# Halved feed-forward products: one more pair per layer, and the last part of layer 1's second projection

## The chip, the cores and the metric

The kernel runs on one core of a Trainium2 chip. The time is device microseconds of one execution. Before the change the runs took 1472.92, 1473.97 and 1474.12 us, a median of 1473.97.

## What is computed

A trunk of two layers on 512 positions of width 1024, all in float32. Each layer normalizes, mixes (a gated convolution with differential attention in layer 0, stick-breaking attention in layer 1), attends to 256 memory positions, and ends in a gated feed-forward part:

```python
def conv_ffn(h, w_up, w_conv, w_down):
    u = causal_dwconv(h @ w_up, w_conv)
    gate, val = jnp.split(u, 2, axis=-1)
    return (jax.nn.silu(gate) * val) @ w_down
...
    x = x + conv_ffn(rmsnorm(x, norm_ffn[l]), ffn_w_up[l], ffn_conv[l], ffn_w_down[l])
```

`w_up` is 1024 x 5632, `w_down` 2816 x 1024, and `w_conv` has width 3 over positions. Only this part is changed.

## The kernel before

Activations lie with features on the 128 partitions and the 512 positions along a row, in tiles ("k tiles") of 128 features. Every float32 operand is carried as two reduced-precision parts, hi (a cast, on ACT) and lo (the rest, a subtraction on DVE, in `split`), and a product is three matmuls: hi with hi, hi with lo, lo with hi.

**Groups.** The weights are cut into groups, listed in the order in which PE uses them by `weight_groups`. In a feed-forward part U0 to U21 are the up-projections: Uj gives one tile of gates and one of values from 8 k tiles. The down-projection is cut by its 22 k tiles into D0 (k tiles 0 to 7, groups D00 to D03 of two output tiles each), D1 (8 to 15, D10 to D13) and D2 (16 to 21, D20 and D21 of four output tiles). `FFN_ORDER` mixes them. A plain U is 2 x 8 x 3 = 48 matmuls of 512 columns; D2 is 8 x 6 x 3 = 144.

**Halved groups.** `lin_halved` takes a U group as a 2 x 2 block product (even and odd k tiles, gate and value, first and second 256 positions) from seven block products instead of eight: 7 x 4 x 3 = 84 matmuls of 256 columns. It needs sums of activations, T, made by `fold`: the scaled activations S of the 8 k tiles and, for each pair of them, two tiles of sums. It also needs sums of weight blocks: the load "a" holds two blocks as they are, "d" one, "b" and "c" sums. The seven products p1 to p7 go to PSUM tiles acc, sc, pv, tr, sc, tr, sc, from which DVE combines the four output quarters c11 to c22 in the tiles u1 and u2. There are 2 sc and 2 tr buffers and one pv, so DVE's reading frees what PE writes next. U7 to U21 of both layers are halved (`SEVEN`); U0 to U5 use unscaled activations and scale the result afterwards (`UP_SCALED`), U6 uses the scaled ones whole.

**Weight sums.** `sums_in_dram` makes b and c ahead of time in DRAM: one copy of the group's four blocks (1 MB, in the queue of SP, "dr<-wts 16x16384"), then three adding copies in POOL's queue (512, 256 and 256 KB). `SUMMED` says after which group each sum is started. `halved_loads` then loads a, d, b, c into the 3 raw buffers; `prep_halved` splits them into the 5 hi and 5 lo buffers (d into sq). SP's queue is in order: a load that waits for a raw buffer holds everything behind it.

**Lo parts by POOL.** For the groups in `LOW` (U2 to U6) lo is not made by DVE: ACT writes the negated hi and POOL adds the weights to it with an adding copy.

**The order.** The program has no fixed order of its own. The class `Issue` plans, when it is built, which instruction of which stream comes next on each engine, from costs (`act`, `tt`, `mm`, `dma`, `add_dma`) and priorities (a smaller number first: 0.9 for the combinations, 1.0 for what follows a product, `FOLD` for fold, 3.0 for loads and splits, `SUMS` for the weight sums). The order of every engine is then fixed in the program.

The end of layer 1: D21's last output tile is added to x and written out in two halves of 256 positions.

Of the kernel before, what the change touches and what calls it, by code (L numbers as in the profile page):

```python
# [17 lines left out]
P = 128  # L18
# [19 lines left out]
UP_SCALED = 6  # L38
FFN_ORDER = [('u', 0), ('u', 1), ('u', 2), ('u', 3), ('u', 4), ('u', 5), ('u', 6), ('u', 7), ('d', 0, 0), ('u', 8), ('d', 0, 1), ('u', 9), ('u', 10), ('d', 0, 2), ('u', 11), ('u', 12), ('d', 0, 3), ('u', 13), ('u', 14), ('u', 15), ('u', 16), ('d', 1, 0), ('u', 17), ('d', 1, 1), ('u', 18), ('d', 1, 2), ('u', 19), ('u', 20), ('d', 1, 3), ('u', 21), ('d', 2, 0), ('d', 2, 1)]
SEVEN = {0: (7, 8, 9, 10, 11, 12, 13, 14, 15, 16, 17, 18, 19, 20, 21), 1: (7, 8, 9, 10, 11, 12, 13, 14, 15, 16, 17, 18, 19, 20, 21)}  # L40

SUMMED = {0: {7: 'A1', 8: 'A1', 9: 'A2', 10: 'A2', 11: 'EO0', 12: 'EO0', 13: 'EO1', 14: 'KV1_0', 15: 'KV3_0', 16: 'Q0_0', 17: 'Q0_0', 18: 'Q1_0', 19: 'XO0_0', 20: 'XO0_0', 21: 'XO1_0'}, 1: {7: 'U17_0', 8: 'U19_0', 9: 'U21_0', 10: 'SQK0', 11: 'SQK0', 12: 'SV0', 13: 'SQK1', 14: 'SQK2', 15: 'SV1', 16: 'SQK3', 17: 'Q0_1', 18: 'Q1_1', 19: 'XO0_1', 20: 'XO1_1', 21: 'U1_1'}}


def weight_groups():
# [22 lines left out]
    def common(l):  # L68
        for a in range(2):
            g.append((f"Q{a}_{l}", "x_w_q", l, ks, c(*range(4 * a, 4 * a + 4))))  # L70
        for a in range(2):
            g.append((f"XO{a}_{l}", "x_w_out", l, ks[4 * a:4 * a + 4], c(*range(8))))

        def up(j):
            g.append((f"U{j}_{l}", "ffn_w_up", l, ks, c(j, 22 + j)))

        def dn(a, b):
            kk = list(range(8 * a, min(8 * a + 8, 22)))
            n = 2 if a < 2 else 4
            g.append((f"D{a}{b}_{l}", "ffn_w_down", l, kk, c(*range(n * b, n * b + n))))  # L80

        for step in FFN_ORDER:
            (up if step[0] == "u" else dn)(*step[1:])
# [21 lines left out]

LOW = {GN[n] for n in ('U2_0', 'U2_1', 'U3_0', 'U3_1', 'U4_0', 'U4_1', 'U5_0', 'U5_1', 'U6_0', 'U6_1')}
# [3 lines left out]
NSLOT = [len(g[3]) * len(g[4]) * P // SLOT for g in GROUPS]  # L110
FIRST = [sum(NSLOT[:i]) for i in range(len(GROUPS) + 1)]
# [38 lines left out]

PREP_FIRST, SUM_FIRST, SUM = 0.45, 3.2, 1.5

FOLD = 1.4

# [51 lines left out]
def vw(x):  # L206
    return x.v() if isinstance(x, T) else x
# [182 lines left out]
def trunk(ctx: ExitStack, tc: tile.TileContext, xT: bass.AP, memT: bass.AP, wts: bass.AP, par: bass.AP, outT: bass.AP):  # L390
# [259 lines left out]
    extra = {}  # L650

    def blocks(gi):

        return wts[FIRST[gi]:FIRST[gi] + 2].rearrange("s p c -> (s p c)").rearrange("(b p c) -> b p c", b=4, p=P)

    summed = {}

    def sums_in_dram(gi, after):

        yield Until(lambda: fin.get(after, 0) > 0)  # L660
        x = blocks(gi)
        d = yield AL(pDR, F32, (4, P, 512))
        yield dma(d.v(), x, 2 * SLOT)
        yield add_dma(d[0:2], x[1:3])
        yield add_dma(d[2], d[0])
        yield add_dma(d[3], d[2])
        summed[gi] = d

    def halved_loads(gi):
        x = blocks(gi)  # L670
        take = [("a", x[0:4:3]), ("r", x[1:3])]
        if gi in ADDED:
            yield Until(lambda: gi in summed)
            d = summed[gi]
            take = [("a", x[0:4:3]), ("d", x[2:3]), ("b", d[1:3]), ("c", d[0:4:3])]
        for n, src in take:
            w = 512 if n == "d" else SLOT
            raw = yield AL(pRAW, F32, (P, w), parts=w // 512)
            v = raw.v().re("p (b c) -> p b c", c=512)
# [25 lines left out]
    def prep_halved(gi):  # L705

        pair = [AL(pHI, F32R, (P, SLOT), parts=2), AL(pLO, F32R, (P, SLOT), parts=2)]
        half = [AL(pSQ, F32R), AL(pSQ, F32R)]
        if gi in ADDED:
            for n in "adbc":  # L710
                yield Until(lambda: (gi, n) in raws)
                r = raws[gi, n]
                h, lo = yield half if n == "d" else pair
                if gi in LOW7 and n in "bc":
                    yield act(h, r)
                    yield act(lo, r, scale=-1.0)
                    src = summed[gi][slice(1, 3) if n == "b" else slice(0, 4, 3)].re("b p c -> p b c")
                    yield add_dma(V(lo, lo.h.rearrange("p (b c) -> p b c", c=512)), src)
# [9 lines left out]
        prepped[gi, "a"] = (ha, la)  # L728
        a11, a12, a21, a22 = r0[:, :512].p(0), r0[:, 512:].p(1), r1[:, :512].p(0), r1[:, 512:].p(1)
        hd, ld = yield half  # L730
# [72 lines left out]

    def lin_halved(gi, N, acc, done):

        st = {}
        t1, t2 = slice(0, 256), slice(256, 512)

        def product(ps, slot, off, rhs, last=True):
            for q in range(4):  # L810
                yield Until(lambda: (gi, slot) in prepped and N.get("folded", 0) > q)
                hi, lo = prepped[gi, slot]
                j = off // 512
                cs = slice(off + q * P, off + (q + 1) * P)
# [31 lines left out]
        def neg(out, a, ps):  # L846
# [5 lines left out]
        then(act(c11, acc[:, :256]), lambda: free(acc), flag("p1"))  # L852
        p2 = yield AL(aSC)
        yield from product(p2[:, :256], "a", 512, part(1, t1))
        p4 = yield AL(aPV)
        yield from product(p4[:, :256], "d", 0, sums(1, t1))
        p6 = yield AL(aTR)
        yield from product(p6[:, :256], "b", 512, sums(1, t2), last=False)
        then(Until(lambda: "p1" in st), sub(c12, c11, p6), lambda: free(p6), flag("p6"),
             add(c11, c11, p2), lambda: free(p2))  # L860
        p5 = yield AL(aSC)
        yield from product(p5[:, :256], "b", 0, sums(0, t1))
# [5 lines left out]
        p3 = yield AL(aSC)  # L868
        yield from product(p3[:, :256], "c", 512, part(1, t2))
        then(Until(lambda: "p5" in st), add(c12, c12, p3), lambda: free(p3), lambda: done(0, u1))  # L870
        fin[gi] = 2
# [591 lines left out]
    def ffn(l, xin, xout, last):  # L1463
        N = norm_x(xin, f"norm_ffn{l}", True)
        acts, own, gate_t = {}, {}, {}

        def fold():

# [9 lines left out]
            for q in range(4):  # L1478
# [4 lines left out]
                for k, b in ((2 * q, b1), (2 * q + 1, b2)):  # L1483
# [9 lines left out]
                    N["S"][k] = (hi, lo)  # L1493
                x, y, z, w = b1[:, t1].p(0), b1[:, t2].p(1), b2[:, t1].p(0), b2[:, t2].p(1)
                yield tt(x, y, x, ALU.subtract)
                yield tt(y, w, y, ALU.subtract)
                yield tt(w, w, x, ALU.subtract)
                yield tt(z, z, w, ALU.subtract)
                for b, (hi, lo) in zip((b1, b2), N["T"][q]):
                    yield from split(hi, lo, b)  # L1500
                free(b1, b2)
# [47 lines left out]
        def dn(a, b):  # L1549
            n = 2 if a < 2 else 4  # L1550
            base = add_x(names[a], names[a + 1], n * b)

            def done(m, ps):
                k = n * b + m
                if last and a == 2 and k == KD - 1:

                    yield Until(lambda: (names[a], k) in F)
                    x = F[names[a], k]
                    for js in (slice(0, S // 2), slice(S // 2, S)):
                        yield tt(x[:, js], x[:, js], ps[:, js], ALU.add)  # L1560
# [309 lines left out]
```

## Time and profile before

| what | value |
|---|---|
| median of the runs | 1473.97 us |
| the profiled execution, its own time | 1473.73 us |
| its span | 1471.9 us |
| granted clock | 1.00 |
| POOL busy | 168.5 us (11%) |
| layer 0, U0 starts, U7 starts, U21 ends | 374.2, 451.3, 689.8 us |
| layer 1, U0 starts, U7 starts, U21 ends, D21 ends | 1119.6, 1196.8, 1435.3, 1468.0 us |
| memory read, written | 239.9, 65.0 MB |

PE is TensorE's matmuls, PEld its weight loads, which overlap them, DVE VectorE, ACT ScalarE, POOL GpSimd, SP SyncE with the queue of the loads. The starts and ends of groups are those of their matmuls in the trace, times are counted from the start of the span, and an operation is written out<-in. q1 is the hardware queue that SP fills, q0 the software queue that POOL fills. DMA shares are of the core's 16 DMA engines. The lines themselves stand in the prediction, where they are used.

### The profile page before, as it was taken

To read this page: it belongs to the slowest core of one execution; us is meant where nothing else is said; L and a number is where in the kernel's file an instruction comes from. 1 tells how busy PE (TensorE), PEld (TensorE's weight loads), DVE (VectorE), ACT (ScalarE), POOL (GpSimd) and SP (SyncE) were. 2 spreads that over 40 slices of the span, in tenths; PEclk is the share of its full clock that TensorE was granted. 3 is DMA by queue.
4 is the path that set the end of the run, shared out by engine and by line. 5 is a ranking of instruction groups with operands and counts; after the bars stand their busy time and mean duration, and the time that the engine had idled before them with its cause. 6 is when DMAs were issued, how large, how long until landed. Compare 5 with 4: busy or idle time off the path is not lost.

```text
span 1471.9 us, 21459 instructions
## 1 busy us (share of the span) xinstructions
PE 1465.0 (100%) x8048; PEld 1272.2 (86%) x8048; DVE 1113.1 (76%) x1891; ACT 810.7 (55%) x1335; POOL 168.5 (11%) x249
## 2 busy tenths in 40 slices
PE   9999999999999999999999999999999999999998
PEld 8888888888889999999888888888888889999897
DVE  7689766665798788867687989967656996888683
ACT  6576546453675445444477877855535854545341
POOL 3212121211210000000111111001101300000000
PEclk9999999999999999999999999999999999999999
DMA  6128898967784445658465463453547954455351
GB/s 237 58 86 243 224 264 269 255 169 161 178 177 143 144 151 170 200 169 227 158 154 147 122 187 79 137 178 107 148 126 219 224 149 128 144 159 184 117 165 57
DMA packets 86088, 243.41 MB, mean 165 GB/s; under 512 B 8064, under 2 KB 8576, under 8 KB 85504
## 3 DMA queue, kind: packets, MB, share of 16 engines
q1 hardware_dynamic: 63744, 200.09, 40.2%
q0 software_dynamic: 22240, 41.95, 17.6%
q8 instruction: 63, 1.03, 0.3%
q14 instruction: 41, 0.34, 0.1%
HBM read 239.91 MB, written 65.01 MB: 207 GB/s over the span
## 4 chain that ended last, share of the span: by engine, by line
PE 95%; DVE 2%; ACT 2%; DMA 1%; issue 1%; SPq 0%; DVEq 0%; ACTq 0%
PE acc L492 67%; PE sc L492 13%; PE pv L492 6%; PE tr L492 6%; PE tr L496 3%; DVE lo L454 0%; ACT h L439 0%; DMA raw<-wts 0%; ACT g L442 0%; DMA x<-xT 0%; DVE g L1619 0%; DVE h L454 0%; DVE g L454 0%; DVE c L454 0%; ACT pt L439 0%
## 5 line engine op out<-in xcount | busy, mean ns | idle before, releaser
L492 PE MATMUL acc<-hs,hi 128*128 128x512 f32 x1568 | 493.7, 392 | 0.0
L439 ACT CAST hi<-raw 128x1024 fp32r<-128x1024 f32 (+1 forms) x294 | 303.3, 1038 | 211.1 <-PE acc L492 79.8
L454 DVE TENSOR_TENSOR lo<-raw,hi 128x1024 fp32r<-128x1024 f32 (+1 forms) x274 | 328.7, 1205 | 90.7 <-ACT hi L439 89.5
L492 PEld LDWEIGHTS acc<-hs,hi 128*128 128x128 f32 x1568 | 292.4, 188 | 57.7
L492 PE MATMUL acc<-hs,lo 128*128 128x512 f32 x784 | 307.5, 392 | 0.0
L492 PE MATMUL acc<-hi,hs 128*128 128x512 f32 x544 | 175.4, 395 | 0.3 <-ACT hs L442 0.3
L492 PEld LDWEIGHTS acc<-hs,lo 128*128 128x128 f32 x784 | 147.3, 188 | 28.7
L492 PE MATMUL acc<-h,hi 128*128 128x512 f32 (+1 forms) x600 | 170.2, 368 | 0.0
L454 DVE TENSOR_TENSOR x<-x,acc 128x512 f32<-128x512 f32 (+1 forms) x105 | 71.2, 680 | 71.4 <-PE acc L492 71.1
L492 PEld LDWEIGHTS acc<-h,hi 128*128 128x128 f32 x600 | 108.2, 189 | 18.1
L462 DVE SCALAR_TENSOR_TENSOR g<-c,pp,g 128x511 f32<-128x511 f32 (+1 forms) x168 | 116.9, 745 | 2.5 <-ACT g L442 2.4
L492 PEld LDWEIGHTS acc<-hi,hs 128*128 128x128 f32 x544 | 100.9, 188 | 20.3 <-ACT hs L442 0.6
L492 PE MATMUL acc<-h,lo 128*128 128x512 f32 (+1 forms) x300 | 109.5, 368 | 0.0
L492 PE MATMUL acc<-lo,hs 128*128 128x512 f32 x272 | 106.8, 393 | 0.0
L492 PE MATMUL acc<-y,hi 128*128 128x512 f32 (+1 forms) x280 | 74.2, 346 | 0.0
L508 POOL DMA_DIRECT2D dr<-wts x30 | 27.4, 913 | 392.1 <-DMA dr<-wts 385.6
L442 ACT ACTIVATE g<-c,pp 128x512 f32<-128x512 f32 x84 | 58.1, 719 | 19.1 <-DVE c L454 18.9
L454 DVE TENSOR_TENSOR g<-g,g 128x512 f32<-128x512 f32 (+2 forms) x112 | 62.9, 568 | 5.0 <-ACT g L439 2.0
L492 PEld LDWEIGHTS acc<-h,lo 128*128 128x128 f32 x300 | 56.6, 189 | 9.4
L442 ACT ACTIVATE g<-sc,rq 128x128 f32<-128x128 f32 (+7 forms) x128 | 61.2, 537 | 5.4 <-PE sc L492 4.9
L508 POOL DMA_DIRECT2D dr<-dr x60 | 50.3, 848 | 115.3 <-DMA dr<-wts 70.1
L492 PEld LDWEIGHTS acc<-lo,hs 128*128 128x128 f32 x272 | 51.2, 188 | 10.0
(241 smaller groups left out, 2672.1 us busy)
## 6 DMA issues: line engine op xcount, KB each, us to landing
raw<-wts SPq DMA_DIRECT2D x226, 512.0 KB, 4.2
raw<-dr SPq DMA_DIRECT2D x60, 512.0 KB, 3.7
dr<-wts POOLq DMA_DIRECT2D x30, 512.0 KB, 6.1
dr<-dr POOLq DMA_DIRECT2D x60, 256.0 KB, 4.7
lo<-wts POOLq DMA_DIRECT2D x20, 512.0 KB, 7.8
raw<-wts SPq DMA_DIRECT2D x38, 256.0 KB, 3.1
x<-xT SPq DMA_DIRECT2D x16, 256.0 KB, 4.7
raw<-memT SPq DMA_DIRECT2D x4, 512.0 KB, 4.5
```

Source lines behind the costliest of these rows:

```text
L439: return nc.scalar.copy(out=out.ap, in_=in_.ap)
L442: return nc.scalar.activation(out=out.ap, in_=in_.ap, func=func, scale=_raw(scale), **kw)
L454: lambda: _ve(eng).tensor_tensor(out=out.ap, in0=in0.ap, in1=in1.ap, op=op))
L462: lambda: nc.vector.scalar_tensor_tensor(out=out.ap, in0=in0.ap, scalar=_raw(scalar), in1=in1.ap, op0=op0, op1=op1))
L492: lambda: nc.tensor.matmul(out.ap, lhsT.ap, rhs.ap, start=start, stop=stop))
L496: return Op("PE", 0.109, [in_, ident_v], [out], lambda: nc.tensor.transpose(out.ap, in_.ap, ident_v.ap))
L508: lambda: nc.gpsimd.dma_start(out=out.ap, in_=i, accum_op=ALU.add, max_dma_last_dim=2048))
```

## The change

1. U6 is halved in both layers, 16 groups of each layer in place of 15, and leaves `LOW`.
2. D2 of layer 1 is four halved groups D20 to D23 in place of two plain ones, each with two output tiles and 6 k tiles: 7 x 3 x 3 = 63 matmuls of 256 columns, 252 together in place of 144 of 512. `fold_down` adds hi and lo of the activations 16 to 21 and makes their sums T (in buffers of kl and pt, free once U6 to U21 are done). The weight blocks have 384 columns (`width`), and their sums are made in DRAM like the others. p5 goes to acc, and p4 of D21 and D23 too. In D23 p2 comes last, and `end` adds to x and writes out the first output tile in two halves.
3. Each layer has its own `FFN_ORDER`. Layer 1 has U17, U18, D11, U19, U20, U21, D12, D13 and then D2.
4. `FOLD` goes from 1.4 to 0.8, and `SUM`, a priority in the norms, from 1.5 to 0.7.
5. `SUMMED` starts the sums at other places. Up to the feed-forward part of layer 0, 12 are started in place of 15; in it 13 (U18 to U21 of layer 0, U6 to U14 of layer 1) in place of 3; between the two parts 3 in place of 12; in layer 1's part 8 (U18 to U21, D20 to D23, after U8 to U13).

```diff
+SEVEN_DOWN = (1,)
+SEVEN = {0: (6, 7, 8, 9, 10, 11, 12, 13, 14, 15, 16, 17, 18, 19, 20, 21), 1: (6, 7, 8, 9, 10, 11, 12, 13, 14, 15, 16, 17, 18, 19, 20, 21)}
...
+DOWN_AFTER = {'D20_1': 'U9_1', 'D21_1': 'U10_1', 'D22_1': 'U12_1', 'D23_1': 'U13_1'}
...
-PREP_FIRST, SUM_FIRST, SUM = 0.45, 3.2, 1.5
-FOLD = 1.4
+PREP_FIRST, SUM_FIRST, SUM = 0.45, 3.2, 0.7
+FOLD = 0.8
...
+    def width(gi):
+        return len(GROUPS[gi][3]) // 2 * P
...
+        p4 = yield AL(aACC if GROUPS[gi][0][:2] == "D2" and GROUPS[gi][0][2] in "13" else aPV)
...
+        p5 = yield AL(aSC if GROUPS[gi][0][0] == "U" else aACC)
...
+        if end is not None:
+            p2 = yield AL(aSC)
+            yield from product(p2[:, :256], "a", 1, part(1, t1))
+            spawn(end(None, p2), 0.8)
...
+        def sums_of(b1, b2, out):
+            t1, t2 = slice(0, 256), slice(256, 512)
+            x, y, z, w = b1[:, t1].p(0), b1[:, t2].p(1), b2[:, t1].p(0), b2[:, t2].p(1)
+            yield tt(x, y, x, ALU.subtract)
+            yield tt(y, w, y, ALU.subtract)
+            yield tt(w, w, x, ALU.subtract)
+            yield tt(z, z, w, ALU.subtract)
+            for b, (hi, lo) in zip((b1, b2), out):
+                yield from split(hi, lo, b)
+
+        def fold_down():
+            yield lin_done(*(f"U{j}_{l}" for j in range(UP_SCALED, 22)))
...
+            for q in range(3):
+                b1, b2 = yield [AL(pC, parts=2), AL(pC, parts=2)]
+                for k, b in ((16 + 2 * q, b1), (17 + 2 * q, b2)):
+                    yield Until(lambda: k in acts)
+                    hi, lo = (vw(x) for x in acts[k])
+                    yield tt(b, hi.f32(), lo.f32(), ALU.add)
+                    ND["S"][k - 16] = acts[k]
+                yield from sums_of(b1, b2, ND["T"][q])
+                free(b1, b2)
+                ND["folded"] = q + 1
...
+            def end(u, p2):
+                k = n * b
+                x = F[names[a], k]
+                t1, t2 = slice(0, 256), slice(256, 512)
+                if p2 is None:
+                    yield tt(x, x, u, ALU.add)
+                    free(u)
+                    F["end"] = True
+                    yield dma(outT[k][:, t2], x[:, t2], 256)
+                else:
+                    yield Until(lambda: "end" in F)
+                    yield tt(x[:, t1], x[:, t1], p2[:, :256], ALU.add)
+                    free(p2)
+                    yield dma(outT[k][:, t1], x[:, t1], 256)
...
+        if l in SEVEN_DOWN:
+            spawn(fold_down(), 1.2)
```

Where rows move, three places. First SP's queue in layer 0 during U13 to U15, with the loads for U15 and U16. Before:

```order
159 L501 DMA raw_5568<-wts 128x2x512
160 L501 DMA raw_5584<-wts 128x512
161 L501 DMA raw_5605<-dr_2655 128x2x512
162 L501 DMA raw_5653<-dr_2655 128x2x512
163 L501 DMA raw_5704<-wts 128x2x512
164 L501 DMA raw_5731<-wts 128x512
165 L501 DMA raw_5759<-dr_2759 128x2x512
166 L501 DMA raw_5792<-dr_2759 128x2x512
167 L501 DMA raw_5841<-wts 128x1024
```

These are a, d, b, c of U15, then of U16, then the first load of D10. With the change, the same loads:

```order
164 L507 DMA raw_5641<-wts 128x2x512
165 L507 DMA raw_5657<-wts 128x512
166 L507 DMA raw_5679<-dr_2755 128x2x512
167 L507 DMA dr_5701<-wts 16x16384
168 L507 DMA raw_5730<-dr_2755 128x2x512
169 L507 DMA raw_5781<-wts 128x2x512
170 L507 DMA raw_5809<-wts 128x512
171 L507 DMA dr_5842<-wts 16x16384
172 L507 DMA raw_5838<-dr_3053 128x2x512
173 L507 DMA raw_5873<-dr_3053 128x2x512
174 L507 DMA raw_5923<-wts 128x1024
```

Two copies for weight sums of layer 1 (U8 and U9, the rows dr<-wts) have come between the loads, one ahead of U15's c and one ahead of U16's b.

Second, DVE where fold ends in layer 0 (pt and rrow are its last sums, acc_4228 and acc_4275 are U6's results, g_4171 and g_4179 the convolutions of U3 and U4). Before:

```order
640 L462 SCALAR_TENSOR_TENSOR g_4360<-acc_4228,pp,g_4360 128x511
641 L454 TENSOR_TENSOR pt_3856<-c_4264,pt_3856 128x512
642 L454 TENSOR_TENSOR hs_4373<-g_4323,hs_4372 128x512
643 L462 SCALAR_TENSOR_TENSOR g_4360<-acc_4228,pp,g_4360 128x510
644 L454 TENSOR_TENSOR rrow_3858<-c_4265,pt_3856 128x512
645 L454 TENSOR_TENSOR lo_4385<-raw_4318,hi_4384 128x1024
646 L454 TENSOR_TENSOR lo_4409<-raw_4339,hi_4408 128x1024
647 L462 SCALAR_TENSOR_TENSOR g_4407<-acc_4275,pp,g_4407 128x511
```

With the change:

```order
619 L468 SCALAR_TENSOR_TENSOR g_4171<-c_4120,pp,g_4171 128x511
620 L460 TENSOR_TENSOR pt_3832<-c_4127,pt_3832 128x512
621 L460 TENSOR_TENSOR rrow_3834<-c_4128,pt_3832 128x512
622 L468 SCALAR_TENSOR_TENSOR g_4171<-c_4120,pp,g_4171 128x510
623 L468 SCALAR_TENSOR_TENSOR g_4179<-c_4169,pp,g_4179 128x511
624 L460 TENSOR_TENSOR g_4171<-g_4171,g_4092 128x512
625 L468 SCALAR_TENSOR_TENSOR g_4179<-c_4169,pp,g_4179 128x510
626 L460 TENSOR_TENSOR c_4217<-acc_4093,rrow_3822 128x512
627 L460 TENSOR_TENSOR h_4225<-g_4171,h_4225 128x512
```

Fold's last two rows have moved from U6's convolutions to those of U3 and U4.

Third, DVE at the end of the program. Before, from the adds of D12 on (lo_14622 is the split of D21's last weights):

```order
1869 L454 TENSOR_TENSOR x_1838<-x_1838,acc_14381 128x512
1870 L454 TENSOR_TENSOR x_1840<-x_1840,acc_14425 128x512
1871 L454 TENSOR_TENSOR x_1842<-x_1842,acc_14443 128x512
1872 L454 TENSOR_TENSOR lo_14622<-raw_14473,hi_14621 128x1024
1873 L454 TENSOR_TENSOR x_1845<-x_1845,acc_14601 128x512
1874 L454 TENSOR_TENSOR x_1852<-x_1852,acc_14606 128x512
1875 L454 TENSOR_TENSOR x_1859<-x_1859,acc_14616 128x512
1876 L454 TENSOR_TENSOR x_1866<-x_1866,acc_14641 128x512
1877 L454 TENSOR_TENSOR x_1872<-x_1872,acc_14662 128x256 x2
```

With the change, from the last product of D20 (sc_14850) to the split of D22's a weights:

```order
1924 L460 TENSOR_TENSOR c_14766<-c_14766,sc_14850 128x256
1925 L460 TENSOR_TENSOR c_14767<-pv_14778,c_14767 128x256
1926 L460 TENSOR_TENSOR x_1838<-x_1838,c_14766 128x512
1927 L460 TENSOR_TENSOR x_1840<-x_1840,c_14767 128x512
1928 L460 TENSOR_TENSOR lo_14848<-raw_14819,hi_14847 128x768
```

and the last rows, all of D23, where tr_15103 is p7, acc_15090 p5, sc_15114 p3, acc_15061 p4 and sc_15125 p2:

```order
1957 L460 TENSOR_TENSOR c_15060<-acc_15090,c_15060 128x256
1958 L460 TENSOR_TENSOR c_15059<-c_15059,sc_15114 128x256
1959 L460 TENSOR_TENSOR c_15060<-acc_15061,c_15060 128x256
1960 L460 TENSOR_TENSOR x_1866<-x_1866,c_15059 128x512
1961 L460 TENSOR_TENSOR x_1872<-x_1872,c_15060 128x512
1962 L460 TENSOR_TENSOR x_1866<-x_1866,sc_15125 128x256
```

Where DVE had an add for each output tile, it now combines products, adds and splits ahead of the next group; and behind the last two products stand five rows in place of two.

More of the change, by code (lines that the diff above doesn't have):

```diff
@@ L109 @@
 HALVED = {GN[f"U{j}_{l}"] for l in SEVEN for j in SEVEN[l]}
-NSLOT = [len(g[3]) * len(g[4]) * P // SLOT for g in GROUPS]
+HALVED |= {GN[f"D2{b}_{l}"] for l in SEVEN_DOWN for b in range(4)}
+DOWN_AFTER = {'D20_1': 'U9_1', 'D21_1': 'U10_1', 'D22_1': 'U12_1', 'D23_1': 'U13_1'}
+ADDED.update({GN[n]: GN[after] for n, after in DOWN_AFTER.items()})
+NSLOT = [-(-len(g[3]) * len(g[4]) * P // SLOT) for g in GROUPS]
 FIRST = [sum(NSLOT[:i]) for i in range(len(GROUPS) + 1)]
@@ L705, in prep_halved @@
     def prep_halved(gi):
-        pair = [AL(pHI, F32R, (P, SLOT), parts=2), AL(pLO, F32R, (P, SLOT), parts=2)]
-        half = [AL(pSQ, F32R), AL(pSQ, F32R)]
+        w = width(gi)
+        pair = [AL(pHI, F32R, (P, 2 * w), parts=2), AL(pLO, F32R, (P, 2 * w), parts=2)]
+        half = [AL(pSQ, F32R, (P, w)), AL(pSQ, F32R, (P, w))]
         if gi in ADDED:
@@ L868, in lin_halved @@
         p3 = yield AL(aSC)
-        yield from product(p3[:, :256], "c", 512, part(1, t2))
-        then(Until(lambda: "p5" in st), add(c12, c12, p3), lambda: free(p3), lambda: done(0, u1))
+        yield from product(p3[:, :256], "c", 1, part(1, t2))
+        then(Until(lambda: "p5" in st), add(c12, c12, p3), lambda: free(p3),
+             (lambda: done(0, u1)) if end is None else (lambda: spawn(end(u1, None), 0.9)))
+        if end is not None:
+            p2 = yield AL(aSC)
+            yield from product(p2[:, :256], "a", 1, part(1, t1))
+            spawn(end(None, p2), 0.8)
         fin[gi] = 2
@@ L1493, in fold @@
                     N["S"][k] = (hi, lo)
[L1494 to L1500, printed above, removed]
+                yield from sums_of(b1, b2, N["T"][q])
                 free(b1, b2)
@@ L1573, in fr @@
                         free(*own[j])
+                    if a == 2 and l in SEVEN_DOWN:
+                        free(*ND["own"])
                 spawn(fr(), 0.1)
```

81 lines of the change are left out of this document (42 added, 39 removed).

## The prediction

> **What bounds the kernel now.** I read the busy times and the chain on the page first, then the waits of PE.
>
> ```profile
> PE 1465.0 (100%) x8048; PEld 1272.2 (86%) x8048; DVE 1113.1 (76%) x1891; ACT 810.7 (55%) x1335; POOL 168.5 (11%) x249
> PE 95%; DVE 2%; ACT 2%; DMA 1%; issue 1%; SPq 0%; DVEq 0%; ACTq 0%
> PE pv L492 <- POOL pt L514: 1.1, 1, 1.1
> PE tr L496 <- DVE pt L454: 0.7, 1, 0.7
> PE sc L492 <- DVE s L1096: 0.5, 1, 0.5
> PE acc L492 <- ACT hs L442: 0.3, 1, 0.3
> PE sc L492 <- ACT g L442: 0.3, 1, 0.3
> ```
>
> PE is 95% of the chain that ended last and waits 2.9 us in all (the last five rows: total, times, longest). So the time is the sum of the matmuls, and anything that makes PE wait is added to it. The feed-forward parts are where the change is made, and there PE has two possible suppliers that could come late: DVE and the weight loads. The stretches of the four products U13 to U16 of layer 0, one row each (engines' busy us, then clock, DMA share, GB/s), behind one row for all of U7 to U21 of that layer:
>
> ```profile
> 451.40:689.80 238.40, 238.40 (x1646) 223.24 (x1645) 184.94 (x282) 111.72 (x149) 5.09 (x6) 1.00 0.56 172
> 555.40:565.50 10.10, 10.10 (x86) 10.10 (x85) 5.61 (x10) 3.53 (x5) 0.00 (x0) 1.00 0.40 131
> 565.50:575.50 10.00, 10.00 (x86) 10.00 (x84) 9.35 (x15) 6.11 (x10) 0.00 (x0) 1.00 0.52 166
> 575.50:585.60 10.10, 10.10 (x87) 10.10 (x86) 10.10 (x18) 6.57 (x10) 0.00 (x0) 1.00 0.62 183
> 585.60:595.70 10.10, 10.10 (x87) 10.10 (x86) 10.10 (x18) 5.77 (x9) 0.00 (x0) 1.00 0.59 176
> ```
>
> In the last two rows DVE (third engine) is busy 10.10 of 10.10 us. These are the places where four products of 10.1 us stand in a row with no down-projection between. A DVE that is held up there has nothing to catch up with, and PE follows closely behind it (DVE rows, and one of PE, us from the start and length):
>
> ```profile
> 576.18 0.42 DVE L454 TENSOR_TENSOR c<-sc,c 128x256 f32<-128x256 f32 x1
> 576.52 0.41 DVE L454 TENSOR_TENSOR c<-c,sc 128x256 f32<-128x256 f32 x1
> 576.94 0.40 PE L492 MATMUL sc<-y,hi 128*128 128x256 f32 x2
> 577.18 1.22 DVE L454 TENSOR_TENSOR lo<-raw,hi 128x1024 fp32r<-128x1024 f32 x1
> 578.31 1.41 DVE L462 SCALAR_TENSOR_TENSOR g<-c,pp,g 128x511 f32<-128x511 f32 x2
> ```
>
> The first row frees an sc buffer at 576.60 and PE writes it at 576.94: 0.34 us to spare. The starts also give the pace of DVE: 0.34 us for a 256-column combination, 1.13 for a split of 1024 columns.
>
> **The columns.** The merged chain gives two prices.
>
> ```profile
> 461.50 12.34 PE acc L492 x60
> 473.84 1.44 PE sc L492 x12
> ```
>
> Twelve matmuls of 256 columns take 1.44 us, 0.120 each. The first row is a D group of 48 matmuls of 512 columns and the first 12 of 256 of the next product: (12.34 - 1.44) / 48 = 0.227. A U group goes from 48 x 0.227 = 10.9 to 84 x 0.120 = 10.1 us, and there are two such U6: -1.6. D2 of layer 1 goes from 144 x 0.227 = 32.7 to 252 x 0.120 = 30.2: -2.5. All together 240 matmuls of 512 columns go (-54.5) and 420 of 256 come (+50.4): **-4.1 us**. A half-width matmul isn't half the price here. The Trainium skill, "TensorE: Matmul & The Clock Gate", section Back-to-back issue gap, gives 518 and 262 cycles for 512 and 256 columns at 2.4 GHz, 216 and 109 ns; by that the sum would be -51.8 + 45.9 = -5.9. The trace's 227 and 120 are both some 11 ns longer, and the change has 180 matmuls more, so the trace decides.
>
> **U6.** Its sums T must exist one product earlier than before. In the new order fold, whose priority went from 1.4 to 0.8, ends on DVE ahead of the convolutions of U4; before, it ended in the middle of those of U6. So T is there more than a product ahead of U6, and what fold pushes back are convolutions and splits of U1 to U5. DVE (third engine) in some two of these products:
>
> ```profile
> 408.00:429.00 21.00, 21.00 (x94) 17.41 (x93) 19.82 (x34) 16.65 (x24) 4.81 (x4) 1.00 0.92 198
> ```
>
> It is busy 19.82 of 21.00 us, so what is pushed back has 1.2 us in these two products to be caught up in. Bounds 0 and 1 us; I take 0, since pushed-back convolutions feed D00 only, four products later.
>
> **The end.** The last rows of the chain before, and the last transfers (KB, us to landing):
>
> ```profile
> 1435.31 32.68 PE acc L492 x144
> 1467.99 0.02 issue
> 1468.02 0.42 DVE x L454
> 1468.44 0.33 DVEq L1865
> outT<-x SPq DMA_DIRECT2D x7, 256.0 KB, 2.0
> outT<-x SPq DMA_DIRECT2D x2, 128.0 KB, 1.7
> ```
>
> Now the product before the last, p3, ends 9 x 0.120 = 1.1 us ahead of PE's end, and behind it DVE has five instructions (its last five in the order shown): 3 x 0.34 for 256 columns and 2 x 0.60 for the adds to x. That ends 1.3 us behind PE. Before, two halves in 0.75 us: **+0.5**. Ahead of that, the split of D22's a weights is the fifth DVE row behind D20's last product. By the matmuls in the order that product ends 31.3 us behind U21, and the DVE rows are 2 x 0.34 + 2 x 0.60 + 0.9 for the split (three quarters of 1.13), with the hand-over 0.2: 34.2. PE asks for it 33.7 + 0.2 us behind U21: **+0.3**. The sums of k tiles 16 to 21 (fold_down) cost DVE per pair two adds of 512, four of 256 and two splits of 512, 4 x 0.60 + 4 x 0.34 = 3.8 us, 11.3 for three; D12 and D13, 21.8 us of PE, stand beside them and use DVE for two adds and two splits each. I count the last pair ready 24.5 us behind U21 against 25.4 needed, so nothing is lost; bounds 0 and 3.
>
> **The weight sums.** Each pair costs one copy of 1.05 MB in the queue of the loads and 1.05 MB of adding copies in POOL's. The rows of the whole run and of U13 to U16 (packets, MB, share of all 16 engines), and the loads of that stretch:
>
> ```profile
> q1 hardware_dynamic: 63744, 200.09, 40.2%
> q0 software_dynamic: 22240, 41.95, 17.6%
> q1 hardware_dynamic: 3168, 6.55, 52.8%
> raw<-dr SPq DMA_DIRECT2D x6, 512.0 KB, 3.6
> raw<-wts SPq DMA_DIRECT2D x5, 512.0 KB, 3.7
> raw<-wts SPq DMA_DIRECT2D x3, 256.0 KB, 3.0
> ```
>
> All engines together take 0.402 x 1471.9 / 200.09 = 2.96 us for a MB of q1 and 6.2 for one of q0, so a sum is 1.05 x 9.1 = 9.6 us of the whole DMA. From U7 to U21 of layer 0 there were three, now 13: 0.56 + 10 x 9.6 / 238 = 0.96. In layer 1 eight come, four of them of three quarters: 0.48 + 0.28 = 0.76. In U13 to U16 of layer 0, about 40 us, four come where none was: 0.53 + 0.95, which doesn't fit. So loads land later there, by how much no row of that place shows. Two other places bound it, U20 to D21 of layer 0 with one sum, and the stretch of EO1 and KV0 with three:
>
> ```profile
> raw<-wts SPq DMA_DIRECT2D x8, 512.0 KB, 5.6
> raw<-wts SPq DMA_DIRECT2D x1, 256.0 KB, 5.7
> q1 hardware_dynamic: 1237, 7.30, 55.9%
> q0 software_dynamic: 1424, 2.69, 45.8%
> raw<-wts SPq DMA_DIRECT2D x7, 512.0 KB, 7.2
> ```
>
> With three raw buffers a late landing becomes a rate. A buffer is held from the issue to the end of the split, landing plus some 2.5 us (cast 1.05, split 1.22, hand-overs), for the half-size d plus 1.4. A U group loads a, d, b, c: at 3.65 and 3.0 that is (3 x 6.15 + 4.4) / 3 = 7.6 us, well inside 10.1. At 5.6 and 5.7: 10.5, 0.4 too long for each U. At 7.2: 12.6, 2.5 too long. Three U groups in a row depend on it (U14 to U16; elsewhere a D with two loads in 10.9 us stands between): 1.2 to 7.5 us in layer 0, and 0 if nothing is late. What queues behind a late split on DVE are the combinations of p5 and p3, which free the sc buffers PE writes 0.34 us later; the first late microsecond therefore reaches PE nearly whole. I take 1.7, near the row with 5.6, which has the same loads, and 0.5 in layer 1 (bounds 0 and 2): **+2.2**.
>
> Sums that leave the stretch between the two feed-forward parts could only take away some of the 2.9 us of waits: -1 to +1, taken as 0.
>
> **Sum:** -4.1 + 0.5 + 0.3 + 2.2 = -1.1 us, from the profiled run's own 1473.73 (0.24 below the median of 1473.97): **1472.6 us**.
>
> **Rivals.**
> - *No load is late in time to matter.* For it: the split in the row at 577.18, of U16's a, ends at 578.40, and PE reads it in U16, from 585.6 on; and the rows of PE's waits show none for a load at U20 and U21, with landings of 5.6. Then -4.1 + 0.8 = -3.3: 1470.4, faster. 0.28.
> - *The transfers are full in U13 to U16, and loads take as long as in the stretch with three sums.* It decides from landings above 5.4 us, where a U's turn of three buffers passes 10.1 us. At 7.2 it costs 7.5 less about 1.5 of lead in layer 0, and 1.5 in layer 1: -3.3 + 7.5 = +4.2, 1477.9, slower. For it: the 0.53 + 0.95 above. Against: in the three-sum stretch q1 still moved 7.30 MB in 34 us, 215 GB/s, against the 183 of the loads alone. 0.20.
> - *Both queues take turns.* A packet of q1 is 3.14 KB and takes 0.149 us of an engine, one of q0 1.89 KB and 0.186 (from the whole run's rows). One each in turn leaves the loads 16 x 3.14 / 0.335 = 150 GB/s. U13 to U16 with copies want 11.5 MB: 7.0 MB in the 47 us that four sums' adding copies last, the rest in 13: 60 us for 40, 12 late after a lead of 8: 1482. The Trainium skill, "DMA: Bandwidth & Descriptors", section Queues, rings and completion order, says that each DMA engine goes round the queues it has work for, a whole packet at a time. The 215 GB/s above speaks against this price: the two shares sum to 1.02, so packets overlap. 0.03.
> - *D2's end hangs on DVE.* If fold_down is 3 us late, all of it is added: -1.1 + 3 = +1.9, 1475.6, no change that can be told. 0.06.
>
> **The numbers.** The forecast's own case, 1471.2 to 1475, has 0.43. A measurement tells 0.2%, 2.95 us, from no change: faster is below 1471.0, slower above 1476.9. Faster: the first rival and a little of the forecast's lower edge, 0.30. Slower: the second and third and the forecast's upper edge, 0.26. Same: 0.44. The range goes from 1469.6 (a gain of 1 us more than the first rival) to 1478.5 (just beyond the second).
>
> **What would show it.** Chain: D2x in four pieces of 7.56 us, U6 in pieces of 1.44. Right: U13 to U16 of layer 0 with DMA share near 1, raw landings between 5 and 6.5, PE's busy time per U up from 10.1 to about 10.7 or waits for DVE of that sum. Wrong to the good: the same share and no PE wait. Wrong to the bad: landings above 7, a longer span from U13 to D10. For the end: last PE matmul to the end of the span 4.4 us in place of 3.9, and a wait at D22's first matmul below 0.5. A stretch between the layers that is longer or shorter by more than 1 us would be outside my working.

## The result and the profile after

The changed kernel takes 1494.62 us, a median of four runs (1490.14 to 1499.15), the kernel before, with a fourth run, 1473.47. The ratio is 1.0143, with a 95% interval from 1.0112 to 1.0175: 21 us slower. The profiled execution took 1494.08 us, its span is 1491.2.

The busy times and the chain by engine, from the page of the changed kernel:

```profile
PE 1467.5 (98%) x8228; PEld 1282.1 (86%) x8228; DVE 1145.1 (77%) x1974; ACT 821.1 (55%) x1357; POOL 177.6 (12%) x263
PE 82%; DMA 9%; DVE 5%; ACT 2%; issue 1%; SPq 0%; DVEq 0%; ACTq 0%
```

and its waits, the two longest of PE, then what DVE's splits and ACT's casts waited for (us in total, times, longest):

```profile
PE sc L498 <- DVE c L460: 15.9, 8, 5.1
PE pv L498 <- POOL pt L520: 1.1, 1, 1.1
DVE lo L460 <- ACT hi L445: 107.9, 77, 5.9
ACT hi L445 <- DMA raw<-dr: 81.2, 39, 5.2
ACT hi L445 <- DMA raw<-wts: 79.5, 47, 5.6
```

PE was 95% of the chain and is 82%; the transfers were 1% and are 9%. A wait that didn't exist before stands first: PE for DVE's combinations at sc, eight times. The two casts' rows are waits for loads of weights ("dr" are the sums from DRAM, "wts" the plain blocks).

The clearest way to see where the time is: the span cut at four matmuls of the trace, the first of U0 of each layer, the first of SQK0 (the first group behind layer 0's feed-forward part), and the last of all. In this table, as in the tables below, FF0 is from U0 of layer 0 to SQK0 and FF1 from U0 of layer 1 to the end of the last matmul.

| us | to U0 | FF0 | between | FF1 | last matmul to span's end |
|---|---|---|---|---|---|
| before | 374.15 | 348.18 | 397.31 | 348.34 | 3.95 |
| after | 374.45 | 360.98 | 396.41 | 354.94 | 4.39 |
| difference | +0.3 | +12.8 | -0.9 | +6.6 | +0.4 |

Both feed-forward parts should have become shorter (by 0.8 and 2.7 us, as the first experiment shows). Against that, FF0 has 13.6 us too many and FF1 9.3.

**Layer 0.** The same 40.3 us that were shown in four pieces, in one piece of the kernel after, and the whole stretch from U7 to U21:

```profile
555.40:595.70 40.30, 32.50 (x267) 31.85 (x265) 27.90 (x46) 18.05 (x25) 7.10 (x9) 0.96 1.05 298
449.30:702.90 253.60, 243.08 (x1659) 226.72 (x1658) 188.77 (x291) 113.53 (x152) 33.08 (x39) 0.99 0.88 252
```

PE is busy 32.5 of 40.3 us, where it was busy for all of it. DVE has fallen from 35.16 to 27.90: it isn't overloaded, it waits. The DMA share is 1.05 in place of 0.53. The longest stall is in U16. First ACT's casts of three loads, then DVE, then PE (start, length, and in brackets the idle time before it with what ended it):

```profile
588.59 1.05 ACT L445 CAST hi<-raw 128x1024 fp32r<-128x1024 f32 x1 [3.99 <-DMA raw<-dr]
592.59 1.04 ACT L445 CAST hi<-raw 128x1024 fp32r<-128x1024 f32 x1 [2.44 <-DMA raw<-dr]
595.26 1.05 ACT L445 CAST hi<-raw 128x1024 fp32r<-128x1024 f32 x1 [1.62 <-DMA raw<-wts]
585.99 0.41 DVE L460 TENSOR_TENSOR c<-c,sc 128x256 f32<-128x256 f32 x1
589.67 1.23 DVE L460 TENSOR_TENSOR lo<-raw,hi 128x1024 fp32r<-128x1024 f32 x1 [3.27 <-ACT hi L445]
590.81 0.68 DVE L460 TENSOR_TENSOR hs<-g,hs 128x512 fp32r<-128x512 f32 x1
591.41 0.41 DVE L460 TENSOR_TENSOR c<-c,tr 128x256 f32<-128x256 f32 x1
593.67 1.23 DVE L460 TENSOR_TENSOR lo<-raw,hi 128x1024 fp32r<-128x1024 f32 x1 [1.84 <-ACT hi L445]
594.81 0.41 DVE L460 TENSOR_TENSOR c<-c,sc 128x256 f32<-128x256 f32 x1
595.14 0.42 DVE L460 TENSOR_TENSOR c<-sc,c 128x256 f32<-128x256 f32 x1
595.61 0.80 PE L498 MATMUL sc<-y,hi 128*128 128x256 f32 x2 [5.13 <-DVE c L460]
```

Read from below: PE waits 5.13 us for the combination at 595.14, which frees an sc buffer. That combination had its operands long ago; it stands in DVE's order behind the two splits at 589.67 and 593.67, for which DVE idled 3.27 and 1.84 us, 5.11 together. They wait for casts, and the casts for loads. These are U16's b and c, which are not needed by PE until later: PE is stopped by weights that it doesn't want yet. The window around it, from 574 to 606 (queues, and the loads with their time to landing):

```profile
q1 hardware_dynamic: 2007, 6.29, 55.5%
q0 software_dynamic: 1333, 2.54, 45.4%
raw<-dr SPq DMA_DIRECT2D x4, 512.0 KB, 8.5
raw<-wts SPq DMA_DIRECT2D x3, 512.0 KB, 8.1
raw<-wts SPq DMA_DIRECT2D x2, 256.0 KB, 4.9
```

Before, such loads took 3.6, 3.7 and 3.0 us in U13 to U16. Both queues together fill the 16 engines.

**Layer 1.** There PE lost most not in U13 to U16, where it was looked for, but in U11 and U12 (4.7 and 2.9 us). The timeline of SP's queue 15 to 30 us ahead of it, and of DVE where it stops:

```profile
1259.55 1.13 SPq L507 DMA_DIRECT2D dr<-wts  x2
1266.46 2.78 SPq L507 DMA_DIRECT2D raw<-dr  x2
1269.29 1.42 SPq L507 DMA_DIRECT2D dr<-wts  x2
1271.34 2.15 SPq L507 DMA_DIRECT2D raw<-wts  x2
...
1287.54 1.23 DVE L460 TENSOR_TENSOR lo<-raw,hi 128x1024 fp32r<-128x1024 f32 x1 [5.15 <-ACT hi L445]
1291.66 1.22 DVE L460 TENSOR_TENSOR lo<-raw,hi 128x1024 fp32r<-128x1024 f32 x1 [1.96 <-ACT hi L445]
```

and the queues and the loads of plain blocks from 1281 to 1309:

```profile
q1 hardware_dynamic: 1923, 5.15, 50.6%
q0 software_dynamic: 1306, 2.38, 48.9%
raw<-wts SPq DMA_DIRECT2D x3, 512.0 KB, 9.1
```

Two sums start after each of U9 and U10 (U19 with D20, U20 with D21), so four copies of together 3.7 MB stand ahead of or between the loads of U11 and U12 within ten us, and their adding copies follow in POOL's queue.

**The clock.** Not all of the loss is waiting. The span is 22.5 us longer than that of e1, the first experiment, which has the same instructions on PE and DVE and a span of 1468.7. PE's waits are 19.2 us in all, against 2.5 in e1, and PE's busy time is 1467.5 us against 1461.7. Three stretches, of U16 in layer 0 and of U11 and U12 in layer 1 (engines' busy us, then granted clock, DMA share, GB/s), and two matmuls of PE ahead of the stall of 5.13 us and two after it:

```profile
589.00:606.00 17.00, 11.87 (x86) 11.66 (x85) 12.95 (x20) 8.41 (x12) 2.53 (x3) 0.80 1.02 277
1281.20:1296.10 14.90, 11.59 (x86) 11.39 (x85) 4.91 (x7) 2.88 (x4) 5.73 (x7) 0.87 1.06 264
1296.10:1309.10 13.00, 11.47 (x86) 11.18 (x86) 10.62 (x17) 7.13 (x10) 2.06 (x5) 0.89 0.93 278
589.60 0.40 PE L498 MATMUL acc<-h,hi 128*128 128x256 f32 x2
596.42 0.63 PE L498 MATMUL sc<-y,hi 128*128 128x256 f32 x2
```

In the trace the granted clock is 0.50 for 6.83 us from 592.43, two us into the stall, and again for 6.83 us from 1292.16. Two matmuls take 0.63 us then, in place of 0.40. PE was at work for 3.65 and 5.5 us of these two times. Half of that, 4.6 us, is an estimate of what the clock took, most of the 5.8 us of busy time: a late load costs the wait, and then slower matmuls.

**The end.** The chain behind D20's last product, and at the end of the program (start, length, what):

```profile
1466.78 0.69 DVE x L460
1467.47 0.88 DVE lo L460
1468.35 0.04 issue
1468.39 1.10 PE acc L498 x7
...
1486.52 0.66 DVE x L460 x2
1487.18 0.09 issue
1487.27 0.79 DVEq L1926
```

PE waits for the split of D22's a, as forecast, 0.57 us in this execution. The last adds end 1.3 us behind the last matmul.

### The profile page after: what moved, and what is told of

Read it like the earlier page. It is cut to its first block, busy times and chain, and to the rows that moved or that the text cites. A ratio compares the mean times of both kernels' runs of the same rounds, so it can differ in the third digit from the quotient of the medians.

```text
span 1491.2 us, 21994 instructions
## 1 busy us (share of the span) xinstructions
PE 1467.5 (98%) x8228; PEld 1282.1 (86%) x8228; DVE 1145.1 (77%) x1974; ACT 821.1 (55%) x1357; POOL 177.6 (12%) x263
## 3 DMA queue, kind: packets, MB, share of 16 engines
q8 instruction: 64, 1.05, 0.3%
## 4 chain that ended last, share of the span: by engine, by line
PE 82%; DMA 9%; DVE 5%; ACT 2%; issue 1%; SPq 0%; DVEq 0%; ACTq 0%
PE acc L498 60%; PE sc L498 10%; DMA raw<-wts 5%; PE pv L498 5%; PE tr L498 4%; DMA raw<-dr 3%; PE tr L502 3%; DVE lo L460 2%; ACT hi L445 1%; DVE c L460 1%; DVE g L468 1%; ACT h L445 0%; ACT g L448 0%; DMA x<-xT 0%; DVE sq L460 0%
## 5 line engine op out<-in xcount | busy, mean ns | idle before, releaser
L445 ACT CAST hi<-raw 128x1024 fp32r<-128x1024 f32 (+2 forms) x302 | 308.7, 1029 | 240.9 <-DMA raw<-dr 81.2
L460 DVE TENSOR_TENSOR lo<-raw,hi 128x1024 fp32r<-128x1024 f32 (+2 forms) x286 | 340.5, 1194 | 109.5 <-ACT hi L445 107.9
L498 PE MATMUL acc<-h,hi 128*128 128x512 f32 (+1 forms) x528 | 145.6, 362 | 0.0
L468 DVE SCALAR_TENSOR_TENSOR g<-c,pp,g 128x510 f32<-128x510 f32 (+1 forms) x176 | 123.1, 746 | 2.0 <-ACT g L448 2.0
L498 PEld LDWEIGHTS acc<-h,hi 128*128 128x128 f32 x528 | 94.5, 190 | 14.6
L460 DVE TENSOR_TENSOR x<-x,acc 128x512 f32<-128x512 f32 x96 | 65.4, 684 | 49.3 <-PE acc L498 48.9
L498 PE MATMUL acc<-h,lo 128*128 128x512 f32 (+1 forms) x264 | 94.6, 361 | 0.4 <-DVE lo L460 0.4
L514 POOL DMA_DIRECT2D dr<-dr x72 | 64.4, 916 | 165.9 <-DMA dr<-wts 112.2
L514 POOL DMA_DIRECT2D dr<-wts x36 | 32.5, 903 | 382.2 <-DMA dr<-wts 381.5
L498 PE MATMUL sc<-y,hi 128*128 128x256 f32 x256 | 51.4, 292 | 15.9 <-DVE c L460 15.9
L445 ACT CAST pt<-tr 128x128 fp32r<-128x128 f32 (+2 forms) x96 | 43.1, 457 | 31.7 <-PE tr L502 31.0
```

The costliest lines, as they stand in the source:

```text
L445: return nc.scalar.copy(out=out.ap, in_=in_.ap)
L460: lambda: _ve(eng).tensor_tensor(out=out.ap, in0=in0.ap, in1=in1.ap, op=op))
L468: lambda: nc.vector.scalar_tensor_tensor(out=out.ap, in0=in0.ap, scalar=_raw(scalar), in1=in1.ap, op0=op0, op1=op1))
L498: lambda: nc.tensor.matmul(out.ap, lhsT.ap, rhs.ap, start=start, stop=stop))
L514: lambda: nc.gpsimd.dma_start(out=out.ap, in_=i, accum_op=ALU.add, max_dma_last_dim=2048))
```

## Experiments

Losses below are differences of FF0 or FF1 to those of the first run, e1, unless said otherwise.

**The sums taken out (e1) and put into the kernel before (e2); one layer at a time (e3, e4).** Only the two tables that start the sums are altered:

```diff
 e1, tables of layer 1 (layer 0: before's, with U6 after A1)
-SUMMED  1: {6: 'U11_0', 7: 'U12_0', 8: 'U13_0', 9: 'U14_0', 10: 'U15_0', ... 18: 'U8_1', 19: 'U9_1', 20: 'U10_1', 21: 'U11_1'}
+SUMMED  1: {6: 'U17_0', 7: 'U19_0', 8: 'U21_0', 9: 'SQK0', 10: 'SQK0', ... 18: 'Q0_1', 19: 'Q1_1', 20: 'XO0_1', 21: 'XO1_1'}
-DOWN_AFTER = {'D20_1': 'U9_1', 'D21_1': 'U10_1', 'D22_1': 'U12_1', 'D23_1': 'U13_1'}
+DOWN_AFTER = {'D20_1': 'KV3_1', 'D21_1': 'SO0', 'D22_1': 'Q1_1', 'D23_1': 'XO0_1'}
 e2: the kernel before, with the change's SUMMED for U7 to U21
 e3: e1, with the change's places for U18 to U21 and D20 to D23
 e4: the change, with U18 to U21 after SQK0 to SQK3, D20 to D23 after SV1, KV1_1, Q1_1, XO0_1
```

> The changed kernel, with only the two tables that start the weight sums altered: between U6 and U21 of both layers only the three sums of the kernel before are left (after U17, U19 and U21 of layer 0), all others start in the attention parts. Theory A (the transfers of the sums delay the weight loads, late loads hold DVE, DVE holds PE): the waits of PE for DVE at sc go from 15.9 us to below 1, the stretch U12 to U17 of layer 0 loses its 13 us and U11 to U15 of layer 1 their 9, and what is left is the sum of the columns and the end, -4.1 + 0.8: about 1470.5. Rival B (the stalls come from DVE's own order: fold and the sums of the norms at a higher priority, U6 and D2 with more instructions for DVE): the waits stay, 1490 to 1495. A would also be wrong if the time came out above 1476: then the sums cost as much in the attention parts.

> The kernel before, with only the table of its weight sums as in the change (U7 to U21; the sums of U6 and D2 don't exist here, so layer 1 has 4 sums in its feed-forward part in place of 8, and layer 0 has 12 in place of 13). Theory A: layer 0 loses about 12 us in U12 to U17, layer 1 less than its 9, some 2 to 4: 1486 to 1490. Rival B: 1473 to 1475.

> The changed kernel, with the sums taken out of layer 0's feed-forward part only (three left there); those of layer 1's part (U18 to U21, D20 to D23) start where the change starts them. Theory A: the stall of layer 0 goes, that of layer 1 (U11, U12, U15: 4.7, 2.9 and 0.8 us) stays: 1494.6 - 13 = 1481 to 1482. If the two layers hang together through something else (B), no such split: 1490 or more, or 1471.

> The changed kernel, with the eight sums taken out of layer 1's feed-forward part only, those of layer 0's part as in the change. Theory A: the stall of layer 0 stays (13 us), that of layer 1 goes: 1494.6 - 8.5 = 1486. B: no change.

| run | us, median | ratio to before, interval | FF0 | FF1 |
|---|---|---|---|---|
| e1 | 1471.43 | 0.9986 (0.9977 to 0.9995) | 347.38 | 345.64 |
| e2 | 1481.66 | 1.0059 (1.0043 to 1.0076) | 355.19 | 349.29 |
| e3 | 1483.73 | 1.0070 (1.0048 to 1.0093) | 347.38 | 355.39 |
| e4 | 1482.71 | 1.0063 (1.0043 to 1.0083) | 358.58 | 345.75 |

e1's busy times and chain, from its page:

```profile
PE 1461.7 (100%) x8228; PEld 1278.2 (87%) x8228; DVE 1146.6 (78%) x1974; ACT 820.4 (56%) x1357; POOL 178.5 (12%) x263
PE 95%; DVE 2%; ACT 1%; DMA 1%; issue 0%; DVEq 0%; SPq 0%; ACTq 0%
```

and its loads from 555 to 597, in U13 to U16 of layer 0:

```profile
raw<-dr SPq DMA_DIRECT2D x7, 512.0 KB, 3.7
raw<-wts SPq DMA_DIRECT2D x6, 512.0 KB, 4.0
```

With the same instructions on PE and DVE as the change, the waits of PE at sc are gone and the loads land in 3.7 to 4.0 us. So it is neither U6, nor D2, nor their sums on DVE, but when the weight sums are made. e2 shows it from the other side, without anything else of the change: FF0 7.0 us longer than before's, FF1 1.0. That is less than the 12 and the 2 to 4 expected, so the loss doesn't simply go by the count of sums. In e3 and e4 each layer has its own loss, 9.8 us in FF1 and 11.2 in FF0. e1 is also the best kernel of the study with all of the change's products: its interval lies below before's time, by 0.7 to 3.4 us (2.1 by the medians, 3.2 by the spans of the two profiled executions).

**The copy in the loads' queue, or the adding copies in POOL's (e5, e6).** Both start from e4; for the nine sums U6 to U14 of layer 1 `sums_in_dram` is cut in two. In e5 the first copies come early, in e6 the adding copies late:

```diff
-        yield Until(lambda: fin.get(after, 0) > 0)
+        yield Until(lambda: fin.get(first, 0) > 0)
         x = blocks(gi)
         d = yield AL(pDR, F32, (4, P, width(gi)))
         yield dma(d.v(), x, 4 * width(gi))
+        yield Until(lambda: fin.get(second, 0) > 0)
         yield add_dma(d[0:2], x[1:3])
```

> As e4 (layer 1's part free, layer 0's part as in the change, which cost 11.0 us of PE in U14 to U17), with the first copy of the nine sums U6 to U14 of layer 1 moved ahead, to EO1 up to XO1 of layer 0; their adding copies in POOL's queue start where the change starts them. Theory A1 (what delays the loads is the 1 MB copy in their own queue, which they stand behind): U14 to U17 lose below 2 us, about 1474. Theory A2 (it is the adding copies, which take turns with the loads): 8 to 11 us are still lost, about 1481. Theory A3 (only the sum of both is more than the transfers can carry: beside adding copies the loads' queue moved 214 GB/s, and the loads want 183 in U13 to U16, the loads with copies 290): below 3 us lost here, and below 3 in the next run too.

> As e4, with the nine copies where the change has them and the adding copies of these nine sums moved behind the feed-forward part (D21 of layer 0 to SO0). A1: 8 to 11 us lost in U14 to U17, about 1481. A2: below 2, about 1473. A3: below 3, 1472 to 1474.

e5 took 1483.94 us and lost 12.5 us in FF0; e6 took 1474.04 and lost 4.5. The queues and loads in 41 us, 565 to 606, of e5:

```profile
q0 software_dynamic: 2282, 4.25, 61.0%
q1 hardware_dynamic: 2988, 6.21, 44.0%
raw<-dr SPq DMA_DIRECT2D x5, 512.0 KB, 6.0
raw<-wts SPq DMA_DIRECT2D x4, 512.0 KB, 6.4
```

and in the same 41 us of e6:

```profile
q1 hardware_dynamic: 3524, 11.67, 78.6%
q0 software_dynamic: 293, 0.53, 8.2%
raw<-wts SPq DMA_DIRECT2D x6, 512.0 KB, 3.9
raw<-dr SPq DMA_DIRECT2D x5, 512.0 KB, 5.8
```

With copies but hardly an adding copy, q1 in e6 moved 11.67 MB in 41 us, 285 GB/s. With adding copies pending all the time, and no 1 MB copy of its own, it moved in e5 6.21 MB, 151 GB/s, less than the 164 that the loads moved in U13 to U16 before. A2 holds: it is mainly the adding copies, and they alone suffice. A3, that only both together are too much, is refuted by e5. The 151 GB/s are not a pure rate, though: in e5's trace q1 has no packet in work for 19% of the window, and by an estimate from its packets it moved some 174 while both queues had any. The copies alone cost 4.5 us, more than the 2 of A2.

**Old priorities (e8).** e1 with `SUM` 1.5 and `FOLD` 1.4.

> As e1 (the sums out of the feed-forward parts, 1471.4), with the two priorities as before the change: SUM 1.5 and FOLD 1.4. The scaled activations then come later, while U6 needs their sums one product earlier. If the priorities are needed for U6: a wait of 2 to 7 us at U6 of each layer, 1475 to 1485. If they are not, since fold has time enough in U0 to U5: 1471.4, no wait at U6.

1483.79 us (ratio 1.0071, 1.0054 to 1.0088): FF0 lost 5.25 us and FF1 5.35, all of it in U6, U7 and D00. So without the two priorities, which e8 took back together, U6 in seven products costs more than it brings.

**U6 alone and D2 alone (e9, e10).** The tables `SEVEN`, `SEVEN_DOWN`, `FFN_ORDER` and `LOW` set so that only one of them is there, sums as in e1.

> Of the change only the sixteenth pair (U6 halved in both layers, the priorities 0.7 and 0.8), D2 plain as before, sums as in e1. If the prices of the columns hold (0.227 and 0.120 us): the last matmul ends 1.6 us earlier than before, 1466.3 in place of 1468.0, time 1471.9. If U6 is held up by its sums T: 1468 or later.

> Of the change only layer 1's D2 as four halved groups with its order, U6 plain as before, sums as in e1. If the prices hold: the last matmul ends 2.5 us less 0.3 to 0.5 (the late split of D22's a) earlier, 1465.8 to 1466.0; from there to the end of the span 4.4 us in place of 3.9; time about 1471.9. If the end hangs on DVE: the last matmul ends at 1467 or later.

| run | us, median | ratio to before, interval | FF0 | FF1 | last matmul to span's end |
|---|---|---|---|---|---|
| e9 | 1472.89 | 0.9997 (0.9988 to 1.0006) | 347.38 | 347.54 | 3.7 |
| e10 | 1472.17 | 0.9991 (0.9981 to 1.0000) | 348.18 | 346.43 | 4.3 |

U6 brings 0.80 us in each part. D2 brings 1.91: 2.4 by the columns (32.68 less 252 x 0.120), less some 0.5 of wait at D22. The last matmul ended at 1469.1 and 1467.9, where 1466.3 and 1465.8 to 1466.0 were expected. e9 came to the first U0 at 377.30 us in place of 374.15. e1, whose orders of PE's matmuls and of SP's queue are the same up to there, came at 374.80, so this isn't the edit. e10 lost 1.0 us up to U0 and 0.8 between the two parts. So both prices are read from FF0 and FF1, and by the medians alone neither edit could be told from no change.

**Fewer at once (e11, e12).** e11 is e3 with D20's and D21's sums after U5 and U7 of layer 1. e12 is e4 with layer 1's U7, U9, U11 and U13 summed behind layer 0's part (its later sums lie a little otherwise there, too).

> As e3 (layer 0's part free; layer 1's part as in the change, where PE lost 4.9 us in U11 and 4.3 in U12), with the sums of D20 and D21 started after U5 and U7 of layer 1, so that they no longer start together with those of U19 and U20. If layer 1 stalls because two sums at a time stand in the queues ahead of U12's loads: the loss in U11 and U12 falls from 9.2 to 1 to 3 us, 1475 to 1477. If any eight sums in that part cost the same: 9 us wherever they stand, 1481 to 1484.

> As e4 (11.0 us lost in U14 to U17 of layer 0), with every other of layer 1's sums (U7, U9, U11, U13) taken out of layer 0's part: nine are left there in place of 13, in U12 to U17 three in place of six. If the loss goes by the number of sums: half, 5 to 6 us, 1477. If it goes by the time in which adding copies are pending, in which the loads get 151 GB/s (e5) in place of 285 (e6): pending half of the time leaves them about 218 for the 235 that loads and copies then want, so 2 to 3 us, 1474.

e11 took 1477.69 us (four runs, 1474.29 to 1480.49); in its profile FF1 lost 10.1 us. U11 and U12 were free of stalls, as expected, but 4.3 us went in U7, where one load of 512 KB took 9.25 us beside D20's adding copy, and 5.6 in U14 to U16. So in that execution the eight sums cost as much as in e3, elsewhere: U11 and U12 weren't the only tight place, as the forecast had it. But it is the slowest of the four; all four are faster than both of e3 (1481.16 and 1486.3), by 6.0 us in the median, and 1477.69 lies between what the two theories gave. Pairs of sums are thus part of layer 1's loss at most, and how large a part isn't shown. e12 took 1472.10 us (0.9989, 0.9979 to 1.0000) and lost 1.8 us in FF0, a little less than the 2 to 3 of the second theory, which went by the time in which adding copies are pending. Nine sums cost 1.8 us there and 13 cost 11.2: not by number. In the last column are the us with the granted clock at 0.50.

| run | sums started in U6 to U21 | lost, us | clock at 0.50, us |
|---|---|---|---|
| before, e1, layer 0 | 3 | 0 | 0 |
| e2, layer 1 (to before) | 4 | 1.0 | 0 |
| e12, layer 0 | 9 | 1.8 | 0 |
| e2, layer 0 (to before) | 12 | 7.0 | 3.4 |
| e4, layer 0 | 13 | 11.2 | 6.8 |
| after, layer 0 | 13 | 13.6 | 6.8 |
| e3, layer 1 | 8 | 9.8 | 6.8 |
| after, layer 1 | 8 | 9.3 | 6.8 |
| e11, layer 1 | 8 (one after U5) | 10.1 | 6.8 |

The large losses are those with the lower clock, which makes them larger still.

## Why the prediction was wrong

**The sign and the size.** 1472.6 us were forecast, 1469.6 to 1478.5 as range, and the time is 1494.6. One term failed: the weight sums, **+2.2** (1.7 and 0.5). They cost 13.6 us in FF0 and 9.3 in FF1.

**The rest of the sum held.** The columns were forecast at -4.1. e1 with e9 and e10 shows -0.80 for each U6 and -1.91 for D2, which is -2.4 and the wait at D22; that wait was forecast at 0.3 and was 0.4 to 0.6. The end was forecast at +0.5 and is +0.4. U6's sums cost nothing with the new priorities, as forecast for that order; e8 shows that with the old ones they would have cost 5.3 us a layer. fold_down was in time: PE has no other wait in D2. The sum without the loads was -3.3; in e1's trace the last matmul ends 3.7 us earlier than before (1464.3 and 1468.0) and the tail is 0.4 longer, -3.2 in all.

**The step that failed: the landing time, taken over from another place.** I took median landings of 5.6 to 7.2 us from two other places, turned them into a turnaround of three raw buffers, charged the excess over 10.1 us to three U groups, and chose the lower end. But neither place had the loads' demand of U13 to U16 beside adding copies that stay pending, here from 580.7 to 596.1. The loads landed in 8.1 and 8.5 us there, beyond the upper row. Landings above 7 us were the prediction's own sign of being wrong to the bad. The turnaround itself was the smaller fault: with 8.5, 8.1 and, for d, 4.9 it gives (2 x 11.0 + 10.6 + 6.3) / 3 = 13.0 us, 2.9 too long for each of three groups, 8.6 together; with the medians of all of U13 to U16, 7.5, 6.2 and 5.9, it is 5.8. U14 to U16 took 11.8, 11.6 and 17.0 us, 10.1 too many, some 1.8 of it the half clock. What was left out is that clock, and U17, behind D10, which took 12.9 us where I had charged nothing.

**How a late load reaches PE.** The turnaround makes an even delay of it, and the trace shows bursts. DVE takes its instructions in the program's order, so one load that lands 5 us late holds everything behind its split, and behind it stands the combination that frees PE's buffer. The 0.34 us to spare, which I had quoted, were the right warning; the row at 595.61 shows 5.11 us of DVE's waits reach PE as 5.13. That a split ends 7 us ahead of PE's reading spoke for the first rival, and was no protection at all.

**Layer 1.** I gave it 0.5 with bounds 0 and 2, from a mean DMA share of 0.76 over the whole part and from U13 to U16. The share of 28 us in U11 and U12 was full: 50.6 and 48.9%. A mean over the whole part hides that. That the sums start there in pairs is part of it at most, by e11.

**The rival with turns.** I had priced it at 150 GB/s for the loads and 12 us for layer 0, and given it 0.03, because q1 had moved 215 GB/s in the stretch with three sums. e5 measured 151 GB/s, and layer 0 lost 11 to 14. That rate didn't speak against turns, for two reasons. Adding copies had packets in work for only 64% of that stretch. And its packets of q1 were large, 7.30 MB in 1237, 5.9 KB each at 0.246 us of an engine; one in turn with one of q0 (0.175 us) gives 16 x 5.9 / 0.421 = 224 GB/s by the rival's own rule. In U13 to U16 they are of 2.07 KB and 0.1075 us, by the same rule 117 GB/s and not 150, for which the mean packet of the whole run had been used. So it is in part luck that 150 is so near e5's 151, in which q1 was also without packets for 19% of the time; and the 12 us contain neither the lower clock nor anything for layer 1. The Trainium skill, "DMA: Bandwidth & Descriptors", section Queues, rings and completion order, says that an engine goes round its queues packet by packet; e5's 151 GB/s beside e6's 285 agree with it. That the packets alternate one for one isn't shown: e5 has 2988 of q1 and 2282 of q0 in the window.

**What stays open.** Why one execution of the change takes 1490 and another 1499. How the late loads would spread with a fourth raw buffer: no run has one. And which wait makes the clock fall: between the first U0 and the last matmul it fell in the change, e2, e3, e4, e5 and e11, whose longest waits of PE were 2.5 to 5.1 us, and in none of the seven others, whose longest were 2.0 or less. But in e4 it also fell after a wait of 1.9 us, and in U17 of the change it didn't after one of 2.6.

## What to carry to other kernels

Before filling a quiet-looking queue, look up what the tightest ten microseconds of its neighbours want, not the mean share of a stage, and count two queues that share engines as one budget. On an engine that works in order, a late operand costs all that stands behind it: ask who waits for the next instruction, not when the late one's result is needed. And count what comes after the wait: here PE worked at half clock for 3.65 and 5.5 us more. And where a rival's price comes out of two measured durations, don't dismiss it by a rate from a stretch in which the cause came and went and the packets were larger.

## What the runs showed of the hardware that wasn't expected

An adding copy in DRAM takes the engines 6 us per MB against 3 for loads and plain copies (e5: 4.25 MB in 61.0% of 41 us; e6: 11.67 MB in 78.6%), and beside adding copies the loads' queue moved 151 GB/s in e5, against 285 in e6 with hardly any. Nine sums' copies lost 4.5 us and their adding copies, which have the same bytes, 12.5 (both beside the four sums of layer 0's own U18 to U21). In the change the granted clock falls to 0.50 some two us into stalls of PE of 5.1 and 3.3 us, and stays there for 6.83 us, well beyond their ends. And the time to the first U0 differs by 2.5 us between executions of programs with the same order of PE and of the loads up to there (374.80 in e1, 377.30 in e9), which is more than either of the two products brings.
